# A decoder trunk in split float32: every second weight chunk's remainder is formed by ScalarE and an accumulating GpSimd DMA instead of VectorE

## The chip, the cores and the metric

The kernel runs on one core of one Trainium2 chip. The metric is the device time of one execution in microseconds (us); the time of a kernel is the median of its runs. Line numbers (L153) are those of the kernel before, unless a row is said to be of the changed kernel.

## What is computed

Four pre-norm residual layers over 512 tokens of width 1024 (pool, conv, attention, pool), each with a branch of width 2048 and a SiLU gate, then a final RMS norm. Cut to what matters:

```python
for i in range(4):                       # pool, conv, mla, pool
    xn = rms_norm(x, norm[i])
    x = x + mixer[i](xn, ...)            # every mixer ends in (y * silu(z)) @ w_out
return rms_norm(x, final_norm)

# pool_mixer:  u, z = split(xn @ w_in, 2); trailing means over 2/4/8/16 tokens minus u,
#              per group @ w_grp, * scale, * silu(z), @ w_out
# conv_mixer:  b, c, h, z = split(xn @ w_in, 4); y = b * conv3(c * h); (y * silu(z)) @ w_out
# mla_mixer:   q, kv latents, rotary key, z from xn @ w_in; 16 heads of causal softmax
#              attention; (o * silu(z)) @ w_out
```

All of it is float32, and nearly all of the work is in the matrix products with the weights.

## The kernel before, in words

Activations lie feature-major in SBUF: 8 tiles of 128 features x 512 tokens. TensorE multiplies in a rounded float32 format (float32r), so each operand is split in two: a rounded half `h` and a remainder `l = raw - h`, and each product is three matmuls, `h*h`, `h*l` and `l*h` (`mm3`, L156 to L159). In the rows the weights are `wh` and `wl`, and the activations `xh`, `xl` or `yh`, `yl`; a row `pz<-xh,wl` writes the PSUM tile pz.

The weights are streamed in chunks of 128 x 1024. `wchunk` (L142) loads one chunk over SP's queue into a raw buffer `wr`, ScalarE writes the rounded half `wh` (L152), VectorE subtracts for the remainder `wl` (L153). There are three buffers each of `wr`, `wh` and `wl`. A chunk feeds 24 matmuls of 128x512. 222 chunks go this way. Another 22, inside attention, are called with `pool=True`: GpSimd does both steps (L149, L150).

I number the 222 chunks from 0 in the order of the code: 0 to 37 are the first pool layer, 38 to 53 its output projection, 54 to 133 the conv layer and its projection, 134 to 155 the input projection of the attention layer, 156 to 169 its output projection, 170 to 221 the last pool layer and its projection.

Beside the splits, VectorE multiplies the norm's factor into the PSUM tiles (L280), forms the mixers' products and splits the activations together with ScalarE (L136, L139). GpSimd forms the running sums of the pool layers (L299: one to four additions for each channel tile, by its window), sums the squares for the norms (L180), and in attention scales the probabilities (L548) and splits those 22 chunks.

The order of instructions on each engine is set by a scheduler, from the program and its own idea of durations; each engine then takes its instructions in that order. The code places one tile by hand: the last gate tile of the attention layer (chunk 155) is issued after the rotary queries, the values and the first head's queries and keys of the first group (`qrope(0)`, `values(0)`, `stage_a(0)`, then `ly.tile`). Its split stands on ScalarE behind the rounded halves of the rotary queries, `qah` and `qbh`.

Of the kernel before, what the change touches and what calls it, by code (L numbers as in the profile page):

```python
# [12 lines left out]
AF = mybir.ActivationFunctionType  # L13
ALU = mybir.AluOpType
# [19 lines left out]
CH = 1024  # L34
WARM = 8

# attention: at which step (head of the group, place within the head's step) the next group's
# values and rotary queries are computed, for the first group and the others
VALUES_AT = ((0, 3), (2, 0), (2, 0))
ROTARY_AT = ((2, 1), (1, 1), (1, 1))  # L40
SPLIT_Y_FROM = 10

# columns of the per-partition parameter array
PC = {}
_n = 0
for _name, _w in (
# [5 lines left out]
    _n += _w  # L52
NPAR = _n

# columns of the constant array
C_ID, C_MASK, C_INV, C_FREQ, C_SIGN, NCON = 0, 128, 640, 704, 705, 706


# [1 line left out]
def trunk_kernel(ctx: ExitStack, tc: tile.TileContext, a):  # L60
# [20 lines left out]
    def f(t):  # L81
        return t.bitcast(F32)

# [1 line left out]
    con = cp.tile([P, NCON], F32, name="con")  # L85
    par = cp.tile([P, NPAR], F32, name="par")
    xt = [xp.tile([P, S], F32, name=f"x{m}") for m in range(KD)]
# [41 lines left out]
    def pcol(name, i):  # L129
        return par[:, PC[name][0] + i : PC[name][0] + i + 1]  # L130

# [1 line left out]
    def split(src, s, eng="act", w=S):  # L133
        h, l = ut(s + "h", F32R, w), ut(s + "l", F32R, w)
        if eng == "act":
# [6 lines left out]
    def wchunk(src, width=CH, pool=False, raw=None):  # L142
        if raw is None:
            raw = wp.tile([P, CH], F32, tag="wr", name=nm("wr"))[:, :width]
            nc.sync.dma_start(raw, src)
        h = wp.tile([P, CH], F32R, tag="wh", name=nm("wh"))[:, :width]
        l = wp.tile([P, CH], F32R, tag="wl", name=nm("wl"))[:, :width]
        if pool:
            nc.gpsimd.tensor_scalar(out=h, in0=raw, scalar1=1.0, scalar2=1.0, op0=ALU.mult, op1=ALU.mult)  # L149
            nc.gpsimd.tensor_tensor(out=l, in0=raw, in1=f(h), op=ALU.subtract)  # L150
        else:
            nc.scalar.activation(h, raw, AF.Copy)  # L152
            nc.vector.tensor_tensor(out=l, in0=raw, in1=f(h), op=ALU.subtract)  # L153
        return h, l

    def mm3(out, ah, al, bh, bl, first, last):  # L156
        nc.tensor.matmul(out, ah, bh, start=first, stop=False)  # L157
# [1 line left out]
        nc.tensor.matmul(out, al, bh, start=False, stop=last)  # L159

    def mtile(out, wh, wl, xs, k0=0, kn=KD, ktot=KD, stride=P, off=0):
        """out += sum over kn k-tiles of w[k].T @ xs[k0 + k]"""
        for k in range(kn):
            c = slice(k * stride + off, k * stride + off + P)
            mm3(out, wh[:, c], wl[:, c], *xs[k0 + k], first=(k0 + k == 0), last=(k0 + k == ktot - 1))

    class Stats:
        """sum of squares over the feature tiles, then the norm's factor of each token"""

        def __init__(self, dim, n):  # L170
            self.dim, self.n, self.i, self.sum = dim, n, 0, None
# [11 lines left out]
                self.parts = split(self.sum, "ss")  # L183

        def rows(self):
            """the factor of token 128 i + p in column i of partition p"""
            st = ps("st")
            for t in self.parts:
                nc.tensor.matmul(st, ones, t, start=(t is self.parts[0]), stop=(t is self.parts[1]))
            v = sp.tile([P, NT], F32, tag="sv", name=nm("sv"))  # L190
            for i in range(NT):
                d = sp.tile([P, P], F32, tag="sd", name=nm("sd"))
                nc.vector.tensor_tensor_reduce(
                    out=d, in0=st[:, i * P : (i + 1) * P], in1=ident, scale=1.0 / self.dim, scalar=EPS,
                    op0=ALU.mult, op1=ALU.add, accum_out=v[:, i : i + 1],
                )
            r = sp.tile([P, NT], F32, tag="sr", name=nm("sr"))
            nc.gpsimd.tensor_tensor(out=r, in0=v, in1=mhalf, op=ALU.pow)
            return r
# [19 lines left out]
            return R  # L219

    class XNorm:
        """xg = x * gain, split, with the statistics of x"""

        def __init__(self, gain):
            self.gain, self.xs, self.st = gain, [], Stats(D, KD)
# [8 lines left out]
                self.st.add(xt[m])  # L234

    class Layer:
        """A layer's first tiles wait in PSUM until the norm's factor is there."""

        def __init__(self, xn, at=(1, 3)):
            self.xn, self.R, self.n, self.posts, self.at = xn, None, 0, [], at  # L240
# [22 lines left out]
        mtile(o, wh, wl, ys, k0=8 * hf, kn=8, ktot=KI)  # L263

    def out_proj(w, ys, gain, o0=None, after=()):
        """x += y @ w, feature-major; the next layer's XNorm (o0: the first half of its first tile)"""
        xn = XNorm(gain)
        for m in range(KD):
            if m == 0 and o0 is not None:
                o = o0  # L270
            else:
                o = ps("o")
                out_half(w, ys, m, 0, o, after=after if m < 2 else ())
            out_half(w, ys, m, 1, o, pool=m == 0 and o0 is not None)
            nc.vector.tensor_tensor(out=xt[m], in0=o, in1=xt[m], op=ALU.add)
            xn.add(m)
        return xn
# [1 line left out]
    def tmul(dst, src, R):  # L279
        nc.vector.tensor_tensor(out=dst, in0=src, in1=R, op=ALU.mult)  # L280

# [1 line left out]
    def pool_layer(j, xn, mid=None, pre=(), at=(1, 3)):  # L283
        win, wg = a[f"pool_in{j}"], a[f"pool_grp{j}"]
        ys = []
# [49 lines left out]
                mid(g)  # L335
        return ys

# [1 line left out]
    def conv_layer(xn):  # L339
        win = a["conv_in"]  # L340
        ys = []
# [37 lines left out]
            ly.tile(win[3 * KI + i], "pz", post_z)  # L379
        return ys  # L380

# [1 line left out]
    def rope_tables():  # L383
        pi = cp.tile([P, S], I32, name="posi")
        nc.sync.dma_start(pi, a["positions"].broadcast_to((P, S)))
# [26 lines left out]
        nc.scalar.activation(cos, t, AF.Sin, scale=-1.0, bias=hp)  # L412
        return cos, sin

# [1 line left out]
    def mla_layer(xn, cos, sin):  # L416
        win = a["mla_in"]
        ly = Layer(xn)
# [7 lines left out]
            (skv if len(lat) <= 2 else sq_).add(t)  # L426

        def post_kr(pl):
            # rotary key, rows [k1, k2, k1, k2]
            kr0, ksw = ut("kr0"), ut("ksw")  # L430
            tmul(kr0, pl, ly.R)
            for q in range(4):
                s = q ^ 1
                nc.sync.dma_start(ksw[32 * q : 32 * q + 32, :], kr0[32 * s : 32 * s + 32, :])
            nc.vector.tensor_tensor(out=kr0, in0=kr0, in1=cos, op=ALU.mult)
            nc.vector.scalar_tensor_tensor(out=ksw, in0=ksw, scalar=con[:, C_SIGN : C_SIGN + 1], in1=sin, op0=ALU.mult, op1=ALU.mult)
            nc.vector.tensor_tensor(out=kr0, in0=kr0, in1=ksw, op=ALU.add)
            kr.extend(split(kr0, "kr"))
# [181 lines left out]
            split_y()  # L620
        return ys, o0, [i.ins for i in last.values()]

# [1 line left out]
    xn = XNorm("pool_norm0")  # L624
    w0, pre = {}, [ps("pu") for _ in range(2)]

# [38 lines left out]
    ys, o0, after = mla_layer(xn, cos, sin)  # L665
    xn = out_proj(a["mla_out"], ys, "pool_norm1", o0, after)

    # last layer: the output projection goes token-major
    xtok = {}

    def turn(g):
# [21 lines left out]


    def token_tile(pos, half, i):
        """the PSUM tiles and columns of token tile i (the very last one comes in two)"""
        if half == 0 or i < NT - 1:
            return [(pos[i], slice(0, S))]
        return [(pos[i + q][:, : S // 2], slice(q * (S // 2), (q + 1) * (S // 2))) for q in range(2)]
# [67 lines left out]


def _layout(i):
    """The inputs in the order in which the chip streams them."""  # L770
    i = {k: np.asarray(v) for k, v in i.items()}

    def cols(v):
        return v.reshape(-1, P).T

    def w_in(w):
        k, n = w.shape
        return w.reshape(k // P, P, n // P, P).transpose(2, 1, 0, 3).reshape(n // P, P, k)

    def w_out(w):  # L780
        return w.reshape(2, 8, P, 8, P).transpose(3, 0, 2, 1, 4).reshape(8, 2, P, CH)

    out = {
        "xT": i["x"][0].T,
        "positions": i["positions"],
        "con": _constants(),
        "par": np.concatenate(
            [cols(i["pool_norm"][0]), cols(i["pool_norm"][1]), cols(i["conv_norm"][0]), cols(i["mla_norm"][0]),
             cols(i["mla_q_norm"][0]), cols(i["mla_kv_norm"][0]), cols(i["pool_scale"][0]), cols(i["pool_scale"][1]),
             *[cols(i["conv_w"][0][q]) for q in range(3)]], axis=1),  # L790
        "final_norm": i["final_norm"][None, :],
        "conv_in": w_in(i["conv_w_in"][0]),
        "conv_out": w_out(i["conv_w_out"][0]),
        "mla_out": w_out(i["mla_w_out"][0]),
        "pool_out0": w_out(i["pool_w_out"][0]),
        "pool_out1": i["pool_w_out"][1].reshape(8, 2, P, 2, S).transpose(3, 0, 2, 1, 4).reshape(2, 8, P, CH),
    }
    for j in range(2):
        out[f"pool_in{j}"] = w_in(i["pool_w_in"][j])
        out[f"pool_grp{j}"] = i["pool_w_grp"][j].reshape(4, 4, P, 2, 2 * P).transpose(0, 3, 2, 1, 4).reshape(4, 2, P, CH)  # L800
    w = i["mla_w_in"][0]
    rope = w[:, QL + KVL : QL + KVL + DR]
    out["mla_in"] = w_in(np.concatenate([w[:, QL : QL + KVL], w[:, :QL], rope, rope, w[:, QL + KVL + DR :]], axis=1))
    q = i["mla_w_q_up"][0].reshape(3, P, H, DN + DR)
    nope = q[..., :DN].reshape(3, P, 8, 2 * P).transpose(2, 1, 0, 3).reshape(8, P, 768)
    rot = q[..., DN:].reshape(3, P, 4, 4, 2, 32).transpose(2, 1, 0, 4, 3, 5).reshape(4, P, 768)
    out["q_up"] = np.concatenate([nope, rot], axis=0)
    kv = i["mla_w_kv_up"][0].reshape(2, P, H, 2, P)
    for n, e in (("k_up", 0), ("v_up", 1)):
        out[n] = kv[:, :, :, e].reshape(2, P, 4, S).transpose(2, 1, 0, 3).reshape(4, P, CH)  # L810
    return {k: np.ascontiguousarray(v) for k, v in out.items()}
# [17 lines left out]
```

## Time and profile before

| | |
|---|---|
| time, median of 3 runs | 1506.08 us (1506.01 to 1506.9) |
| span of the profiled execution, first to last instruction | 1504.8 us |
| profiled execution's own time outside its span | not given; the median of the runs lies 1.3 us above the span |
| TensorE matmuls busy | 1490.4 us, 6712 matmuls |
| VectorE, ScalarE, GpSimd busy | 779.5, 495.0, 305.2 us |
| mean granted TensorE clock | 0.995 |

How to read the rows. A group row has line, engine, operation, written and read tiles (buffer numbers left out), shapes, count, then busy us and mean ns of one, then the idle time of the engine just before them and what ended it. A timeline row has the start (us from the span's start), the duration in us, engine, line, operation, tiles, count, and in brackets the idle time before it and what ended that. A row of waits has the waiting engine and line, the one it waited for, the us in total, how often, and the longest. PE is TensorE's matmuls, PEld its weight loads, DVE VectorE, ACT ScalarE, POOL GpSimd, SP the queue that issues loads. A row of windows has the stretch, its length, the busy time of the five engines with the number of their instructions, then the granted clock, the mean share of the DMA engines that was busy, and GB/s.

### The profile page before, as it was taken

What the parts mean: (1) busy time and instruction counts of PE and PEld (TensorE: products, weight loads), DVE (VectorE), ACT (ScalarE), POOL (GpSimd) and SP (SyncE); (2) the same over time, 40 slices, a digit from 0 to 9 for tenths busy, and PEclk for the clock granted to TensorE, in tenths of its full rate; (3) what the DMA queues carried; (4) which work ended last, traced back from release to release, by engine and by line L of the source; (5) the groups of instructions that cost most, each with busy time, mean ns of one, the idle gap of its engine ahead of it and who ended that gap; (6) DMA issues with size and microseconds to landing.
All of it is one profiled execution on the core that took longest, in us unless ns stands there. A gap on an engine that the chain in (4) does not pass through costs nothing.

```text
span 1504.8 us, 17426 instructions
## 1 busy us (share of the span) xinstructions
PE 1490.4 (99%) x6712; PEld 1221.1 (81%) x6712; DVE 779.5 (52%) x1250; ACT 495.0 (33%) x772; POOL 305.2 (20%) x312
## 2 busy tenths in 40 slices
PE   9999999999999999999999999899999999999998
PEld 7888888888888888888888878788888888888887
DVE  4665454335554555556345545666643455545442
ACT  5333233322222222223232424445632233333331
POOL 2223320111000000000101035445711111134010
PEclk9999999999999999999999999999999999999999
DMA  6233323233333333333233232223123333323331
GB/s 214 85 98 98 98 93 92 96 97 95 90 96 98 99 86 97 98 98 98 88 95 105 82 94 69 67 75 81 43 85 98 91 92 98 88 95 99 100 111 56
DMA packets 42659, 140.49 MB, mean 93 GB/s; under 512 B 5584, under 2 KB 5584, under 8 KB 42576
## 3 DMA queue, kind: packets, MB, share of 16 engines
q1 hardware_dynamic: 41712, 137.81, 30.3%
q10 hardware_dynamic: 864, 1.57, 0.3%
q8 instruction: 52, 0.85, 0.2%
q14 instruction: 31, 0.25, 0.1%
HBM read 132.80 MB, written 2.10 MB: 90 GB/s over the span
## 4 chain that ended last, share of the span: by engine, by line
PE 97%; DVE 1%; issue 0%; ACT 0%; DMA 0%; SPq 0%; POOLq 0%; POOL 0%; ACTq 0%
PE pz L159 8%; PE pz L157 8%; PE pz L158 8%; PE o L157 6%; PE o L158 6%; PE o L159 6%; PE pu L159 4%; PE pu L157 4%; PE pu L158 4%; PE pb L159 2%; PE pc L159 2%; PE ph L159 2%; PE pm L158 2%; PE pm L159 2%; PE pm L157 2%; PE ph L157 2%
## 5 line engine op out<-in xcount | busy, mean ns | idle before, releaser
L152 ACT ACTIVATE wh<-wr 128x1024 fp32r<-128x1024 f32 x222 | 235.4, 1060 | 699.7 <-issue 183.1
L153 DVE TENSOR_TENSOR wl<-wr,wh 128x1024 fp32r<-128x1024 f32 x222 | 298.5, 1345 | 226.3 <-ACT wh L152 226.1
L159 PE MATMUL pz<-xh,wl 128*128 128x512 f32 x512 | 201.8, 394 | 0.3 <-DVE wl L153 0.3
L157 PE MATMUL pz<-xh,wh 128*128 128x512 f32 x512 | 201.5, 394 | 0.0
L158 PE MATMUL pz<-xl,wh 128*128 128x512 f32 x512 | 200.9, 392 | 0.0
L157 PE MATMUL o<-yh,wh 128*128 128x512 f32 x384 | 151.4, 394 | 0.0
L159 PE MATMUL o<-yh,wl 128*128 128x512 f32 x384 | 151.2, 394 | 0.0
L158 PE MATMUL o<-yl,wh 128*128 128x512 f32 x384 | 151.1, 393 | 0.0
L159 PEld LDWEIGHTS pz<-xh,wl 128*128 128x128 f32 x512 | 96.1, 188 | 22.9 <-DVE wl L153 0.7
L158 PEld LDWEIGHTS pz<-xl,wh 128*128 128x128 f32 x512 | 96.3, 188 | 22.5
L157 PEld LDWEIGHTS pz<-xh,wh 128*128 128x128 f32 x512 | 96.1, 188 | 21.9
L159 PE MATMUL pu<-xh,wl 128*128 128x512 f32 x255 | 100.6, 396 | 0.3 <-DVE wl L630 0.3
L157 PE MATMUL pu<-xh,wh 128*128 128x512 f32 x255 | 100.6, 399 | 0.0
L158 PE MATMUL pu<-xl,wh 128*128 128x512 f32 x255 | 100.5, 395 | 0.0
L180 POOL TENSOR_TENSOR sq<-sq,sq 128x512 f32<-128x512 f32 x25 | 42.0, 1681 | 264.6 <-ACT sq L175 264.2
L299 POOL TENSOR_TENSOR s<-u 128x527 f32<-128x527 f32 x32 | 37.4, 1169 | 267.8 <-DVE u L280 247.3
L280 DVE TENSOR_TENSOR sz<-pz,R 128x512 f32<-128x512 f32 x64 | 42.4, 687 | 87.7 <-PE pz L159 87.7
L159 PEld LDWEIGHTS o<-yh,wl 128*128 128x128 f32 x384 | 72.2, 188 | 16.7
L158 PEld LDWEIGHTS o<-yl,wh 128*128 128x128 f32 x384 | 72.2, 188 | 16.5
L157 PEld LDWEIGHTS o<-yh,wh 128*128 128x128 f32 x384 | 72.2, 188 | 16.4
L367 POOL TENSOR_TENSOR yb<-yb,R 128x512 f32<-128x512 f32 x16 | 20.7, 1293 | 309.9 <-DVE yb L366 309.9
L299 POOL TENSOR_TENSOR s<-s 128x525 f32<-128x525 f32 (+2 forms) x48 | 63.9, 1331 | 3.8
(229 smaller groups left out, 2839.8 us busy)
## 6 DMA issues: line engine op xcount, KB each, us to landing
wr<-in_conv_in SPq DMA_DIRECT2D x64, 512.0 KB, 3.6
wr<-in_pool_in SPq DMA_DIRECT2D x62, 512.0 KB, 3.7
wr<-in_pool_out SPq DMA_DIRECT2D x32, 512.0 KB, 3.7
wr<-in_mla_in SPq DMA_DIRECT2D x22, 512.0 KB, 3.6
wr<-in_pool_grp SPq DMA_DIRECT2D x16, 512.0 KB, 3.6
wr<-in_conv_out SPq DMA_DIRECT2D x16, 512.0 KB, 3.7
wr<-in_mla_out SPq DMA_DIRECT2D x16, 512.0 KB, 3.7
wr<-in_q_up SPq DMA_DIRECT2D x12, 384.0 KB, 3.1
```

Source lines behind the costliest of these rows:

```text
L152: nc.scalar.activation(h, raw, AF.Copy)
L153: nc.vector.tensor_tensor(out=l, in0=raw, in1=f(h), op=ALU.subtract)
L157: nc.tensor.matmul(out, ah, bh, start=first, stop=False)
L158: nc.tensor.matmul(out, ah, bl, start=False, stop=False)
L159: nc.tensor.matmul(out, al, bh, start=False, stop=last)
L180: eng.tensor_tensor(out=self.sum, in0=self.sum, in1=sq, op=ALU.add)
L280: nc.vector.tensor_tensor(out=dst, in0=src, in1=R, op=ALU.mult)
L299: nc.gpsimd.tensor_tensor(out=nx[:, lo:], in0=cur[:, lo:], in1=cur[:, lo - d : S + PAD - d], op=ALU.add)
L367: nc.gpsimd.tensor_tensor(out=y, in0=y, in1=ly.R, op=ALU.mult)
```

## The change

`wchunk` counts its calls. For every second chunk (1, 3, ... 221; 111 of the 222), ScalarE writes the rounded half as before, then the same copy with the sign turned into `wl` (`scale=-1.0`), and GpSimd issues a DMA that adds the raw chunk onto `wl` in SBUF: `-h + raw` is the remainder. VectorE has no part in these chunks. The even chunks and those with `pool=True` are split as before.

```diff
         if pool:
             nc.gpsimd.tensor_scalar(out=h, in0=raw, scalar1=1.0, scalar2=1.0, op0=ALU.mult, op1=ALU.mult)
             nc.gpsimd.tensor_tensor(out=l, in0=raw, in1=f(h), op=ALU.subtract)
+        elif acc[0] % 2:
+            acc[0] += 1
+            nc.scalar.activation(h, raw, AF.Copy)
+            nc.scalar.activation(l, raw, AF.Copy, scale=-1.0)
+            nc.gpsimd.dma_start(f(l), raw, accum_op=ALU.add)
         else:
+            acc[0] += 1
             nc.scalar.activation(h, raw, AF.Copy)
             nc.vector.tensor_tensor(out=l, in0=raw, in1=f(h), op=ALU.subtract)
         return h, l
+
+    acc = [0]
```

In the changed kernel the lines behind are eight higher: an even chunk has its rounded half on L158 and its subtraction on L159, an odd one L153 (rounded half), L154 (sign-turned copy) and L155 (the DMA); the matmuls are L165 to L167. Several comments fall away too.

The scheduler orders every engine anew. ScalarE before, around the split of chunk 155 (`wh_6380`; qah and qbh are the rotary queries' rounded halves, vh, qh and kh those of values, queries and keys):

```order
L136 ACTIVATE qah_6263<-t_1122_6255 128x512
L136 ACTIVATE qbh_6267<-t_1123_6256 128x512
L152 ACTIVATE wh_6380<-wr_6378 128x1024
L136 ACTIVATE vh_6304<-pv_6297 128x512
L136 ACTIVATE vh_6315<-pv_6308 128x512
```

And ScalarE at the same place of the changed kernel (chunk 155 is `wh_6457`, `wl_6458`):

```order
L136 ACTIVATE qah_6340<-t_1122_6332 128x512
L136 ACTIVATE qbh_6344<-t_1123_6333 128x512
L154 ACTIVATE wl_6458<-wr_6455 128x1024
L153 ACTIVATE wh_6457<-wr_6455 128x1024
L136 ACTIVATE vh_6381<-pv_6374 128x512
```

The split keeps its place behind `qbh`, with the sign-turned copy ahead of the rounded half. On GpSimd the DMA of that chunk stands behind the last of the four `pool=True` splits that come before it, in the changed kernel:

```order
L149 TENSOR_SCALAR wh_6420<-wr_6418 128x768
L150 TENSOR_TENSOR wl_6421<-wr_6418,wh_6420 128x768
L149 TENSOR_SCALAR wh_6426<-wr_6424 128x1024
L150 TENSOR_TENSOR wl_6427<-wr_6424,wh_6426 128x1024
L155 DMA wl_6458<-wr_6455 128x1024
L149 TENSOR_SCALAR wh_6568<-wr_6566 128x1024
```

Between those two splits (the ends of the piece) there was nothing before. The second place is the first pool layer, GpSimd before, the running sums of two neighbouring channel tiles (`u_747` is the input of a tile, `s` its sums):

```order
L299 TENSOR_TENSOR s_617<-s_615 128x525
L293 MEMSET u_747 128x16
L299 TENSOR_TENSOR s_750<-u_747 128x527
L299 TENSOR_TENSOR s_752<-s_750 128x525
L293 MEMSET u_794 128x16
```

And there in the changed kernel (`wl_853` is chunk 13, `wl_922` chunk 15, `u_752` the same input):

```order
L155 DMA wl_853<-wr_850 128x1024
L301 MEMSET u_752 128x16
L307 TENSOR_TENSOR s_755<-u_752 128x527
L155 DMA wl_922<-wr_919 128x1024
L307 TENSOR_TENSOR s_757<-s_755 128x525
L301 MEMSET u_800 128x16
```

The transfer of chunk 15 stands behind the first addition of this tile. The transfer of chunk 11 stands in the same way behind the second addition of an earlier one. TensorE's order differs in a few places only. The one that matters here is the group mix at the end of the first pool layer, TensorE before (`plh_1654` is the last channel tile, pm the products of the mix, which begins 13 matmuls ahead of the first row with `plh_1654`):

```order
L158 MATMUL pm_1819<-pll_1414,wh_1796 128x512
L159 MATMUL pm_1819<-plh_1413,wl_1797 128x512
L157 MATMUL pm_1819<-plh_1464,wh_1796 128x512
L157 MATMUL pm_1800<-plh_1654,wh_1796 128x512
L158 MATMUL pm_1819<-pll_1465,wh_1796 128x512
```

And in the changed kernel, where the same tile is `plh_1670`:

```order
L165 MATMUL pm_1882<-plh_1618,wh_1858 128x512
L166 MATMUL pm_1882<-pll_1619,wh_1858 128x512
L167 MATMUL pm_1882<-plh_1618,wl_1859 128x512
L165 MATMUL pm_1818<-plh_1670,wh_1814 128x512
L165 MATMUL pm_1837<-plh_1670,wh_1814 128x512
L165 MATMUL pm_1863<-plh_1670,wh_1858 128x512
L165 MATMUL pm_1882<-plh_1670,wh_1858 128x512
```

All matmuls with the last channel tile have moved to the end of the mix, 36 matmuls behind its start.

## The prediction

> **What bounds the kernel now.** I read the page's engine totals first, then what TensorE waits for, then single chunks on the timeline. The totals:
>
> ```profile
> span 1504.8 us, 17426 instructions
> PE 1490.4 (99%) x6712; PEld 1221.1 (81%) x6712; DVE 779.5 (52%) x1250; ACT 495.0 (33%) x772; POOL 305.2 (20%) x312
> ```
>
> TensorE is busy for all but 14.4 us of the span. Whatever leaves VectorE (52%) shortens nothing unless TensorE waits for it, so the next view is the waits of TensorE alone:
>
> ```profile
> PE s L534 <- ACT kh L136: 4.9, 1, 4.9
> PE warm L127 <- DVE dummy L89: 1.4, 1, 1.4
> PE pu L655 <- DVE xl L231: 0.6, 1, 0.6
> PE pu L159 <- DVE wl L630: 0.3, 1, 0.3
> PE pz L159 <- DVE wl L153: 0.3, 1, 0.3
> ```
>
> Only the last of these rows is line 153, the line that the change removes from half the chunks: one wait of 0.3 us. The largest, 4.9 us in attention, ends on line 136, which the change leaves alone, and no changed chunk lies near it (the chunks there are split on GpSimd with pool=True). So the change can save some 0.3 us, and the question is what it puts at risk: how long before its first use is a remainder finished today? One ordinary odd chunk, number 53 (the last of pool_out0), ScalarE, VectorE and TensorE rows of the timeline:
>
> ```profile
> 303.88 1.06 ACT L152 ACTIVATE wh<-wr 128x1024 fp32r<-128x1024 f32 x1 [3.35 <-issue]
> 304.98 1.23 DVE L153 TENSOR_TENSOR wl<-wr,wh 128x1024 fp32r<-128x1024 f32 x1 [3.65 <-ACT wh L152]
> ...
> 314.95 0.40 PE L157 MATMUL o<-yh,wh 128*128 128x512 f32 x1
> 315.18 0.40 PE L158 MATMUL o<-yl,wh 128*128 128x512 f32 x1
> 315.42 0.39 PE L159 MATMUL o<-yh,wl 128*128 128x512 f32 x1
> ```
>
> ScalarE may start once TensorE has left the third-last chunk (three buffers of each kind); TensorE reaches the new remainder two chunks later, at 315.42: 11.5 us after ScalarE's start, of which 2.3 are used (303.88 to 306.21). The same distance holds through the projections; I looked for the odd chunks where it is shorter.
>
> **What the change does, term by term.** 111 of 222 remainders leave VectorE: 111 x 1.345 us = 149 us by the first row here, which lie beside TensorE's work and save nothing. 111 copies of the second row's kind are added, 111 x 1.06 = 118 us, on an engine that is 33% busy. And 111 transfers are queued on GpSimd, each behind its copy.
>
> ```profile
> L153 DVE TENSOR_TENSOR wl<-wr,wh 128x1024 fp32r<-128x1024 f32 x222 | 298.5, 1345 | 226.3 <-ACT wh L152 226.1
> L152 ACT ACTIVATE wh<-wr 128x1024 fp32r<-128x1024 f32 x222 | 235.4, 1060 | 699.7 <-issue 183.1
> ```
>
> Call A the time from the transfer's issue on GpSimd to its landing. An ordinary chunk then needs 1.06 + 1.06 + 0.1 (my allowance for the hand-over) + A of its 11.5 us, so an A up to 9.3 us is hidden by the two chunks that TensorE works on meanwhile; beyond that TensorE waits. The raw buffer is held until the transfer lands, but its next load needs only 3.6 us and is wanted three chunks (3 x 24 matmuls of 0.23, 16.6 us) after the start: that breaks at 16.6 - 2.2 - 3.6 = 10.8, later than 9.3.
>
> No row has an accumulating transfer or one from GpSimd. The nearest are these (KB each, median us to landing):
>
> ```profile
> wr<-in_conv_in SPq DMA_DIRECT2D x64, 512.0 KB, 3.6
> wr<-in_q_up SPq DMA_DIRECT2D x12, 384.0 KB, 3.1
> qrs<-qah SPq DMA_DIRECT2D x16, 64.0 KB, 2.0
> ```
>
> The lower bound is 2.0 us, an SBUF to SBUF copy of an eighth of the size. From 384 to 512 KB a load grows by 0.5 us, so 512 KB are about 2.0 us of moving and 1.6 of fixed time. An addition reads 512 KB twice and writes it once: with the two reads in series 1.6 + 2 x 2.0 = 5.6 us. Three whole passes of a load, 3 x 3.6 = 10.8 us, are the upper bound. I take A = 5.6 as an estimate, nearest to the load row with its moving part doubled.
>
> The Trainium skill bears on this: "Collectives: The Full Stack" (The bandwidth ceiling) says that the adding in a DMA is free and the second source read halves the rate, and "DMA: Bandwidth & Descriptors" (Anatomy of one DMA) gives 2.0 us plus bytes over 436 GB/s for a GpSimd-issued transfer. For 1.05 MB read that is an estimate of 4.4 us, and the sum below would come to 1510.5; its formula gives 3.2 us for a plain 512 KB where the trace's loads take 3.6, and no row here shows an addition.
>
> With A = 5.6 the ordinary chunks stay hidden. Where is the cover thinner? **Chunk 155**, the last gate tile of the attention layer, is split late, because on ScalarE it stands behind the rotary queries:
>
> ```profile
> 895.86 0.63 ACT L136 ACTIVATE qbh<-t 128x512 fp32r<-128x512 f32 x1 [1.36 <-DVE t L503]
> 896.40 1.05 ACT L152 ACTIVATE wh<-wr 128x1024 fp32r<-128x1024 f32 x1
> ...
> 897.48 1.23 DVE L153 TENSOR_TENSOR wl<-wr,wh 128x1024 fp32r<-128x1024 f32 x1 [0.26 <-ACT wh L152]
> ...
> 898.76 0.50 PE L159 MATMUL pz<-xh,wl 128*128 128x512 f32 x1 [0.31 <-DVE wl L153]
> ```
>
> It arrives exactly when used. In the changed order ScalarE writes the sign-turned copy first (896.40 to 897.45), then the rounded half (to 898.5). GpSimd has nothing before the transfer at that time:
>
> ```profile
> 889.97 2.72 POOL L150 TENSOR_TENSOR wl<-wr,wh 128x1024 fp32r<-128x1024 f32 x1
> 904.00 1.05 POOL L149 TENSOR_SCALAR wh<-wr 128x1024 fp32r<-128x1024 f32 x1 [11.32 <-PE pz L158]
> ```
>
> So it is issued at 897.55 and lands at 897.55 + A; TensorE, whose order here is the same, moves from 898.76 by A - 1.2 = **4.4 us**. What stands behind it in TensorE's order waits with it. The GpSimd split at 904.00 waits for this tile and moves along; so do the rotary work and the 4.9 us wait of the next group, which begin from TensorE's own matmuls.
>
> A pause this long has a second price, the clock. The windows around the existing 4.9 us wait (PE busy, then the other engines, the granted clock third from the end):
>
> ```profile
> 940.00:945.00 5.00, 1.02 (x10) 0.78 (x8) 4.30 (x4) 0.76 (x2) 4.92 (x3) 0.90 0.08 21
> 945.00:950.00 5.00, 4.03 (x9) 2.73 (x10) 4.42 (x8) 2.15 (x6) 0.87 (x1) 0.50 0.33 79
> 950.00:955.00 5.00, 5.00 (x31) 4.65 (x30) 2.83 (x13) 2.45 (x8) 2.08 (x4) 0.92 0.44 105
> ```
>
> While TensorE worked again, the clock was at half for 4.03 us of the middle window and short by 8% of the last: 2.0 + 0.4 = 2.4 us lost. A pause of 4.7 us (4.4 and the 0.31 there already) is nearly as long as that one, and one case is all the trace has; I take half the price, **1.2 us**.
>
> "TensorE: Matmul & The Clock Gate" in the Trainium skill (Part 1: The HAM clock gate) says that the clock halves after one whole free-running window of about 3.4 us without work; the 4.9 us wait agrees. By it an estimate of (4.7 - 3.4) / 3.4, some 4 in 10, would hit, near the half that I took.
>
> **Chunk 15**, a gate tile of the first pool layer, is the second thin place. GpSimd now has its transfer behind the first addition of a running sum, whose input comes late:
>
> ```profile
> 93.26 1.06 ACT L152 ACTIVATE wh<-wr 128x1024 fp32r<-128x1024 f32 x1 [0.96 <-PE pz L158]
> ...
> 99.01 1.06 POOL L299 TENSOR_TENSOR s<-u 128x527 f32<-128x527 f32 x1 [16.43 <-PE pz L159]
> ...
> 104.78 0.40 PE L159 MATMUL pz<-xh,wl 128*128 128x512 f32 x1
> ```
>
> Issue at 100.07 instead of 95.5, used at 104.78: 4.7 us of cover, so a wait of 5.6 - 4.7 = **0.9 us**. The next are chunk 159 (split at 1112.92, used at 1121.46: 8.54 - 2.22 = 6.3 us of cover) and chunk 11 (behind an addition that ends at 76.19, used at 82.64: 6.4); both hold at 5.6.
>
> ```profile
> 1112.92 1.06 ACT L152 ACTIVATE wh<-wr 128x1024 fp32r<-128x1024 f32 x1 [2.64 <-PE o L158]
> 1121.46 0.39 PE L159 MATMUL o<-yh,wl 128*128 128x512 f32 x1
> 75.13 1.06 POOL L299 TENSOR_TENSOR s<-s 128x525 f32<-128x525 f32 x1
> 82.64 0.40 PE L159 MATMUL pu<-xh,wl 128*128 128x512 f32 x1
> ```
>
> The other way round, GpSimd's additions queue behind transfers that wait for their copies. That reaches TensorE only at the end of a pool layer, where today the sums of the last channel tile end at 216.5 and the group mix begins at 220.65; the matmuls of that tile now stand 36 matmuls (8.3 us at 0.23 each) into the mix, so some 9 us of delay would be covered after the 3 us that VectorE and ScalarE need. I cost it at nothing.
>
> ```profile
> 214.07 2.43 POOL L299 TENSOR_TENSOR s<-s 128x521 f32<-128x521 f32 x2
> 220.65 0.39 PE L157 MATMUL pm<-plh,wh 128*128 128x512 f32 x1
> ```
>
> More traffic on the DMA engines is no bound by itself: the queue that carries the weights fills 30.3% of them, and 111 transfers of twice a load's reads add about as much again.
>
> ```profile
> q1 hardware_dynamic: 41712, 137.81, 30.3%
> ```
>
> **Sum.** 4.4 + 1.2 + 0.9 = 6.5 us. The profiled execution spans 1504.8 us; the median of the runs, 1506.08, lies 1.3 above it, for what lies around the span. 1504.8 + 6.5 + 1.3 = **1512.6 us**. A measurement of this kernel can tell about 0.2% (3.0 us) from no change.
>
> **Rivals.**
> - *A quick addition, no change to be told.* If A is 2.0 to 3.9 us, chunk 155 costs 0.8 to 2.7 and the pause is under 3.1, well short of the one that cost the clock, so I add no price for it: 1506.9 to 1508.8. For it speaks that both ends are in SBUF, as in the 2.0 us row; against it that 512 KB from memory take 3.6. This ends on the other side, not slower. Decided at A = 3.9.
> - *A slow addition that sets the pace.* Above 9.3 us ordinary chunks wait too. A chunk that waited gives the next odd one more room (its buffer was released before the wait), so about every second of the 111 pays: at the bound of 10.8, 55 x 1.5 = 83 us, with some 20 of the thin places about 1610. For it: three passes could be made one after the other; against it: the load row needs only 2.0 us of moving per pass.
> - *Faster.* The 4.9 us wait ends on a chain of VectorE steps of which one takes 2.76 us, where the group before takes 0.67 for the same (the chain that ended last, start and length):
>
> ```profile
> 894.57 0.67 DVE qal L139
> 940.22 2.76 DVE qal L139
> ```
>
>   If the shift undoes that stretch, the wait gives back some 2 us and its 2.4 us of clock. With A = 2.0 (0.8 us) that is 1506.1 + 0.8 - 4.4 = 1502.5. Against it: that chain and the GpSimd splits beside it both start from TensorE, so their overlap should repeat.
>
> **How the numbers follow.** Forecast (A from 3.9 to 9.3) 0.63, quick 0.18, slow 0.15, faster 0.04. The forecast's upper end at A = 9.2: 8.0 at chunk 155, 4.5 at 15, 2.9 at 159, 2.8 at 11, and the clock's 2.4 at both longest pauses: 23.0 us, 1529.1. The range goes from the quick case's 1506.9 to there, 1507 to 1529; the slow and the faster case, about 2 in 10, are left out. Faster by over 0.2%: 0.04; within 0.2%: 0.18; slower: 0.63 + 0.15 = 0.78.
>
> **What would show it.** Right: the waits of TensorE hold one new row near 898 us, on line 159 for a transfer of wl, of about 4.7 us; the DMA issues show wl from GpSimd at 5 to 6 us to landing; near 105 us a wait of about 1 us; elsewhere none. Wrong: a landing time below 3.9 or above 9.3; waits on ordinary chunks, on the sums of the pool layers, or on ScalarE's rounded halves; or a 4.9 us wait that has changed its length.

## The result, and the profile after

The changed kernel takes **1516.00 us** (median of 3 runs, 1515.41 to 1516.73) where the kernel before takes 1506.08. The ratio is 1.0064, with a 95% interval of 1.0044 to 1.0083: 9.9 us slower. The forecast was 1512.6. From here on, lines are those of the changed kernel.

The totals and two of the DMA queues of the page of the changed kernel:

```profile
span 1514.7 us, 17696 instructions
PE 1492.3 (99%) x6712; PEld 1223.1 (81%) x6712; DVE 619.0 (41%) x1139; ACT 599.6 (40%) x883; POOL 391.6 (26%) x423
...
q1 hardware_dynamic: 41712, 137.81, 27.8%
q0 software_dynamic: 15984, 58.20, 20.4%
```

VectorE lost 160 us of work, ScalarE gained 105 and GpSimd 86; none of that is the cost, as the runs below show. The waits of TensorE (waiting line, what it waited for, us in total, times, longest):

```profile
PE s L542 <- ACT kh L136: 4.9, 1, 4.9
PE pz L167 <- DMA wl<-wr: 4.1, 1, 4.1
PE warm L127 <- DVE dummy L89: 1.5, 1, 1.5
PE pu L661 <- DVE wh L637: 0.7, 1, 0.7
PE pz L165 <- ACT wh L153: 0.4, 1, 0.4
```

111 transfers, and one wait for one of them. It is chunk 155, on the timeline of ScalarE, GpSimd and TensorE:

```profile
896.36 1.04 ACT L154 ACTIVATE wl<-wr 128x1024 fp32r<-128x1024 f32 x1
897.31 1.04 ACT L153 ACTIVATE wh<-wr 128x1024 fp32r<-128x1024 f32 x1
...
897.70 0.89 POOL L155 DMA_DIRECT2D wl<-wr  x1 [5.06 <-ACT wl L154]
...
898.40 0.50 PE L165 MATMUL pz<-xh,wh 128*128 128x512 f32 x1 [0.44 <-ACT wh L153]
898.73 0.40 PE L166 MATMUL pz<-xl,wh 128*128 128x512 f32 x1
903.22 0.79 PE L167 MATMUL pz<-xh,wl 128*128 128x512 f32 x1 [4.09 <-DMA wl<-wr]
903.81 0.63 PE L165 MATMUL pz<-xh,wh 128*128 128x512 f32 x1
```

The copy, the issue, 5.5 us from 897.70 to the first matmul at 903.22, and then matmuls of 0.63 to 0.79 us where the row before the wait has 0.40: the clock has halved. The windows behind the wait (PE busy first, the granted clock third from the end):

```profile
900.00:905.00 5.00, 1.78 (x4) 1.49 (x5) 2.54 (x5) 1.26 (x3) 0.00 (x0) 0.60 0.78 161
905.00:910.00 5.00, 5.00 (x17) 3.95 (x16) 0.00 (x0) 0.00 (x0) 0.00 (x0) 0.71 0.53 149
```

1.78 us at half speed lose 0.9, 5.00 us at 0.71 lose 1.45: together about 2.3 us of clock. So this one place costs some 6.4 us.

The rest is behind the last matmul. The last output is issued on ScalarE's queue; first the row of before, whose span ends at 1504.8, then that of after, which ends at 1514.7:

```profile
1501.28 0.34 ACTq L752 DMA_DIRECT2D out<-fo  x1
```

```profile
1507.42 0.34 ACTq L760 DMA_DIRECT2D out<-fo  x1
```

3.5 us from there to the end before, 7.3 us after: 3.8 us more, with no kernel instruction in them. The trace names it. Every engine meets the others at the end, and GpSimd arrives last, because its closing drain instruction takes 7.95 us where it took 1.03. The rows of before and after (the line that the end of the program is put down to, POOLq for GpSimd's sequencer, how many, the shortest, median and longest in ns, first and last start):

```profile
L825 POOLq DRAIN  x3: 39/77/1034, 1499.5 to 1504.5; - x3
```

```profile
L833 POOLq DRAIN  x3: 34/102/7952, 1505.7 to 1514.1; - x3
```

In both kernels the last of the other engines, SP, arrives 4.5 us after this drain begins (1504.07 against 1499.53 before, 1510.20 against 1505.67 after). So 1.03 us of drain were hidden, and 7.95 stand out by 3.4; the other 0.4 of the 3.8 lie behind the meeting, and their cause is not shown.

6.4 and 3.8 are 10.2; smaller shifts of both signs take 0.3 back. Matched by their number in TensorE's order, the matmuls of the changed kernel start 0.9 us early at 118 us of the kernel before, 1.2 late at 672 and level with it at 895, just ahead of chunk 155. So the transfers up to there cost nothing on balance. The DMA issues (KB each, median us to landing) give the price that had no row before:

```profile
wl<-wr POOLq DMA_DIRECT2D x111, 512.0 KB, 4.5
wr<-in_conv_in SPq DMA_DIRECT2D x64, 512.0 KB, 3.8
wr<-in_pool_in SPq DMA_DIRECT2D x62, 512.0 KB, 4.3
```

### The profile page after: what moved, and what is told of

Its sections match the earlier page's. It is cut to its first block, busy times and chain, and to the rows that moved or that the text cites. A ratio compares the mean times of both kernels' runs of the same rounds, so it can differ in the third digit from the quotient of the medians.

```text
span 1514.7 us, 17696 instructions
## 1 busy us (share of the span) xinstructions
PE 1492.3 (99%) x6712; PEld 1223.1 (81%) x6712; DVE 619.0 (41%) x1139; ACT 599.6 (40%) x883; POOL 391.6 (26%) x423
## 3 DMA queue, kind: packets, MB, share of 16 engines
q0 software_dynamic: 15984, 58.20, 20.4%
## 5 line engine op out<-in xcount | busy, mean ns | idle before, releaser
L158 ACT ACTIVATE wh<-wr 128x1024 fp32r<-128x1024 f32 x111 | 117.6, 1060 | 309.7 <-issue 271.2
L155 POOL DMA_DIRECT2D wl<-wr x111 | 97.2, 876 | 551.2 <-ACT wl L154 512.1
L153 ACT ACTIVATE wh<-wr 128x1024 fp32r<-128x1024 f32 x111 | 117.6, 1059 | 306.9 <-issue 123.9
L167 PE MATMUL pz<-xh,wl 128*128 128x512 f32 x512 | 202.6, 396 | 4.1 <-DMA wl<-wr 4.1
L165 PE MATMUL pz<-xh,wh 128*128 128x512 f32 x512 | 202.1, 395 | 0.4 <-ACT wh L153 0.4
L159 DVE TENSOR_TENSOR wl<-wr,wh 128x1024 fp32r<-128x1024 f32 x111 | 137.6, 1240 | 118.8 <-ACT wh L158 118.7
L165 PE MATMUL o<-yh,wh 128*128 128x512 f32 x384 | 151.1, 394 | 0.0
L167 PE MATMUL o<-yh,wl 128*128 128x512 f32 x384 | 150.9, 393 | 0.0
L154 ACT ACTIVATE wl<-wr 128x1024 fp32r<-128x1024 f32 x111 | 115.8, 1043 | 13.7 <-PE po L166 13.7
L167 PEld LDWEIGHTS pz<-xh,wl 128*128 128x128 f32 x512 | 96.6, 189 | 26.7 <-DMA wl<-wr 4.5
L165 PEld LDWEIGHTS pz<-xh,wh 128*128 128x128 f32 x512 | 96.6, 189 | 22.7 <-ACT wh L153 0.9
L165 PE MATMUL pu<-xh,wh 128*128 128x512 f32 x255 | 100.2, 397 | 0.0
L167 PE MATMUL pu<-xh,wl 128*128 128x512 f32 x255 | 100.1, 394 | 0.0
L167 PEld LDWEIGHTS o<-yh,wl 128*128 128x128 f32 x384 | 72.2, 188 | 16.8
L165 PEld LDWEIGHTS o<-yh,wh 128*128 128x128 f32 x384 | 72.1, 188 | 16.7
L283 DVE TENSOR_TENSOR x<-o,x 128x512 f32<-128x512 f32 x24 | 16.6, 692 | 167.7 <-PE o L167 167.7
```

What stands on the lines that cost most here:

```text
L154: nc.scalar.activation(l, raw, AF.Copy, scale=-1.0)
L155: nc.gpsimd.dma_start(f(l), raw, accum_op=ALU.add)
```

## The experiments

The theory: chunk 155 costs 6.4 us (wait and clock), the closing drain 3.8, and the other 110 transfers nothing. The main rival: the cost is spread over all transfers. In each run the kernel before was timed on the same chip; its median there was 1506.52 us for the first four runs below, 1505.91 for the next four and 1506.27 for the last four.

### Chunk 155 kept on VectorE

```diff
-        elif acc[0] % 2:
+        elif acc[0] % 2 and acc[0] != 155:
```

> As changed, but chunk 155 alone is split on VectorE again. Theory: the change costs 4.2 us of wait and about 2.2 us of clock at chunk 155, and 3.8 us behind the last output, where GpSimd's closing drain takes 7.95 us instead of 1.03; the other 110 transfers cost nothing. Then the wait on line 167 near 898 us is gone and the time falls by 6.4 from 1516.0 to 1509.6, with the long closing drain still there. Rival (the 9.9 us are spread over the 111 transfers, by contention with the loads): 110/111 of the cost stays, about 1515.9. Rival (the closing drain is a consequence of the late chunk): about 1506.

Measured: **1509.39 us**, ratio 1.0019 (1.0010 to 1.0028). With one chunk of 111 changed back, 2.9 us are left of the 9.9 (1509.39 against 1506.52). The wait is gone, the drain is still 7.87 us. The theory holds; a cost spread evenly over the transfers, which would have left 1515.9, is excluded.

### Chunk 155 alone

```diff
-        elif acc[0] % 2:
+        elif acc[0] == 155:
```

> Only chunk 155 goes by ScalarE and the accumulating DMA; all others as before. Theory: this one transfer holds nearly the whole cost: 4.2 + 2.2 at TensorE and 3.8 at the end, 1506.1 + 10.2 = 1516.3. Rival (the closing drain grows with the number of transfers): the 3.8 shrinks to 3.8/111, 1512.5. Rival (cost spread over all transfers): 1506.2.

Measured: **1513.74 us**, ratio 1.0050 (1.0037 to 1.0062). This is neither 1516.3 nor 1506.2. The wait is there in full:

```profile
PE pz L167 <- DMA wl<-wr: 4.3, 1, 4.3
...
PE pz L165 <- ACT wh L153: 0.5, 1, 0.5
```

But the drain takes 1.13 us and the end 3.5: the drain does grow with the transfers, as the first rival had it. 7.2 us are the price of the wait (4.3 and 0.5, less the 0.3 that was there before), of the clock, and about half a microsecond of small shifts. The 7.2 us of chunk 155 alone and the 2.9 us of all the others add up to 10.1, close to the 9.9 of the whole change.

### Chunk 3 alone

```diff
-        elif acc[0] % 2:
+        elif acc[0] == 3:
```

> Only chunk 3 goes by the accumulating DMA, some 1450 us before the end and well covered. Theory: no matmul waits for it, but the closing drain of GpSimd is as long as with 111 transfers: 1506.1 + 3.8 = 1509.9. Rival (the drain is long only because transfers are recent at the end, or many): 1506.1, drain about 1 us.

Measured: 1506.81 us, ratio 1.0001 (0.9993 to 1.0010), drain 1.13 us. The theory of a fixed price at the end falls. A single well-covered transfer costs nothing that can be told.

### The sign-turned copies without the DMA

```diff
-            nc.gpsimd.dma_start(f(l), raw, accum_op=ALU.add)
+            nc.vector.tensor_tensor(out=l, in0=raw, in1=f(l), op=ALU.add)
```

> As changed, with ScalarE's sign-turned copy, but VectorE adds the raw chunk onto it in place of the DMA. It measures the 111 extra copies of ScalarE alone. Theory: they cost only at chunk 155, where the remainder is ready at about 897.45 + 0.1 + 1.24 = 898.8 as before and the rounded half is 0.4 us late: 1506.1 to 1506.6, closing drain 1 us. Rival (the longer row of ScalarE delays chunks elsewhere, and the slow drift of 2 us over the conv layer comes from it): 1508 or more.

Measured: 1506.65 us, ratio 1.0001 (0.9992 to 1.0010), drain as before. 111 extra copies on ScalarE, 104 us of work, are free; of what the theory named, only the 0.4 us wait for the rounded half of chunk 155 shows.

### A plain copy in place of the addition

```diff
-            nc.gpsimd.dma_start(f(l), raw, accum_op=ALU.add)
+            nc.gpsimd.dma_start(f(l), raw)
```

> As changed, chunk 155 included, but the transfers copy the raw chunk over the sign-turned copy and add nothing, so the remainder is left out: wl holds the raw chunk. It prices the addition. If the second read takes time, the landing falls from 4.5 us to that of a load, 3.6 to 4.3, and the wait at chunk 155 from 4.1 to about 3.2: 1516.0 - 0.9 = 1515.1, or 1512.9 if the shorter pause spares the clock its 2.2. Rival (the addition is free, and the 4.5 are what any 512 KB transfer of GpSimd takes): landing, wait and time unchanged, 1516.0.

Measured: 1516.69 us, ratio 1.0073 (1.0058 to 1.0088). The forecasts of 1515.1 and 1512.9 are missed. The time alone would say that the addition is free; the trace says otherwise. Its queue and its issues:

```profile
q0 software_dynamic: 15984, 58.20, 9.7%
...
wl<-wr POOLq DMA_DIRECT2D x111, 512.0 KB, 2.9
```

The same bytes hold the DMA engines half as long (9.7% against 20.4%), and a transfer lands 1.6 us sooner (2.9 against 4.5). The Trainium skill's rule on the second source read ("Collectives: The Full Stack", The bandwidth ceiling: twice the read traffic for each byte written) agrees with both rows. The wait at chunk 155 is 2.7 us, 1.4 less, but two things take that back. The closing drain is 10.12 us, longer than with the addition, and the end 9.4 instead of 7.3. And the shorter pause did not spare the clock:

```profile
900.00:905.00 5.00, 3.13 (x7) 2.48 (x8) 2.58 (x5) 1.31 (x3) 0.00 (x0) 0.60 0.56 160
905.00:910.00 5.00, 5.00 (x17) 3.97 (x16) 0.03 (x1) 0.00 (x0) 0.13 (x1) 0.72 0.49 132
```

After 2.7 us of pause the clock is at 0.60 and 0.72, as after 4.1. The shorter pause even pays more: TensorE works for 3.13 us of the first window instead of 1.78, and loses 1.6 there and 1.4 in the second, 3.0 us instead of 2.3. "TensorE: Matmul & The Clock Gate" in the Trainium skill (Part 1: The HAM clock gate) asks for an idle window of about 3.4 us. Here a pause of 2.7 was enough, with one of 0.44 and two matmuls just ahead, so the measurement decides. The three differences sum to 1.4 us more, yet the span is only 0.2 longer: behind the 4.9 us wait in attention the lead of the matmuls over the changed kernel grows from 0.7 to 2.0 us.

### A second transfer behind each first

```diff
-        elif acc[0] % 2:
+        elif acc[0] % 2 and acc[0] != 155:
...
             nc.gpsimd.dma_start(f(l), raw, accum_op=ALU.add)
+            nc.gpsimd.dma_start(f(l), f(l))
```

> As changed with chunk 155 on VectorE, and behind each of the 110 adding transfers a second one that copies the remainder onto itself, so that a remainder lands after 4.5 + 0.1 + some 4.4 = 9.0 us. It tests the cover of 9.3 us that the prediction gave to an ordinary chunk. Theory: the conv layer still shows no wait of TensorE for a remainder; chunk 159 (cover 6.3) and chunk 11 (6.4) wait some 2.7 and 2.6, and the pool layers lose a little by a GpSimd that waits for the first transfer: 1509.4 + 5 to 12 = 1514 to 1521. Rival (the cover is really 8 us or less): about every second of some 100 ordinary chunks waits 1 us or more, over 1560.

Measured: **1566.86 us**, ratio 1.0411 (1.0394 to 1.0428). The forecast of 1514 to 1521 is missed, and by the time alone the rival won. But the second transfer was slower than I had put it, 5.3 us and not 4.4, as the issues show; beside them the first waits of TensorE:

```profile
wl<-wr POOLq DMA_DIRECT2D x110, 512.0 KB, 4.6
wl<-wl POOLq DMA_DIRECT2D x110, 512.0 KB, 5.3
```

```profile
PE pz L168 <- DMA wl<-wl: 15.0, 19, 3.2
PE po L167 <- DMA wl<-wl: 7.3, 2, 5.9
PE s L543 <- ACT kh L136: 4.8, 1, 4.8
PE o L168 <- DMA wl<-wl: 4.6, 10, 0.8
PE pm L168 <- DMA wl<-wl: 3.4, 2, 1.7
PE pu L168 <- DMA wl<-wl: 3.2, 4, 1.5
```

One ordinary chunk of the conv layer, ScalarE, GpSimd and TensorE rows of its timeline:

```profile
392.66 1.06 ACT L153 ACTIVATE wh<-wr 128x1024 fp32r<-128x1024 f32 x1 [1.49 <-PE pc L167]
...
394.96 0.87 POOL L155 DMA_DIRECT2D wl<-wr  x1 [5.99 <-ACT wl L154]
399.86 0.56 POOL L156 DMA_DIRECT2D wl<-wl  x1 [4.02 <-DMA wl<-wr]
...
404.97 0.50 PE L168 MATMUL pz<-xh,wl 128*128 128x512 f32 x1 [0.61 <-DMA wl<-wl]
```

404.97 - 394.96 = 10.0 us to landing against a cover of 9.3, and TensorE waits 0.61. The nineteen waits on `pz` average 0.8. So the cover of 9.3 us is right within a few tenths (10.0 less the wait is 9.4), and the time is what a landing of 10 does to it: the waits on these transfers sum to 34 us of the 54.7 by which the span has grown. PE is busy 1506.7 us instead of 1490.4. Little of that is the clock: its mean is 0.994 against 0.995, some 1559.5 x 0.006 - 1504.8 x 0.005 = 1.8 us. The first matmul behind a wait has a longer row (0.50 above, where the usual is 0.39), which is part of the rest; what else is in it is not shown. Above its kernel before, this run lies 60.9 us, the one with the 110 first transfers alone 2.9.

### How the closing drain grows: none late, late ones only, every fourth, all

```diff
-        elif acc[0] % 2:
+        elif acc[0] % 2 and acc[0] < 210 and acc[0] != 155:
```

> As changed, but chunk 155 and the six odd chunks of the last projection (211 to 221) are split on VectorE: 104 transfers, the last some 60 us before the end. The run with chunk 3 alone showed no long closing drain, that with 110 transfers did: number or nearness? If nearness to the end makes the drain long: drain about 1 us, 1506 (1505 to 1506.5). If the number does: as with 110 transfers, 1509.4.

```diff
-        elif acc[0] % 2:
+        elif acc[0] % 2 and acc[0] >= 210:
```

> Only the six odd chunks of the last projection (211 to 221) go by the adding transfer. If nearness to the end makes the closing drain long: 1506.5 + 3.4 = 1509.9, drain about 8 us. If the number does: 1506.5, drain 1 us.

Measured: **1509.00 us**, ratio 1.0020 (1.0010 to 1.0030), drain 7.38, and 1506.77 us, ratio 1.0006 (0.9996 to 1.0015), drain 1.54. It is the number (or the bytes, since all transfers have one size), not the nearness to the end.

```diff
-        elif acc[0] % 2:
+        elif acc[0] % 4 == 1:
```

> Every fourth chunk (1, 5, ... 221; 56 of 222, chunk 155 not among them) goes by the adding transfer, the others as before. So far GpSimd's closing drain took 1.03 us without transfers, 1.13 with 1, 1.54 with 6, 7.38 with 104, 7.87 with 110: some 0.062 us for each. The last output lands 4.7 us after the drain begins, so the drain is hidden up to (4.7 - 1.0) / 0.062 = 59 transfers. Theory: 56 give a drain of 4.5 us and cost nothing: 1506 (1505 to 1506.8). Rival (each transfer costs its 0.03 us of the 3.4 whatever the drain is beside): 1506.4 + 1.7 = 1508.1.

Measured: **1510.26 us**, ratio 1.0024 (1.0015 to 1.0034), a miss of both forecasts. The drain is 5.63 us, not 4.5: 0.082 us for each of the 56, so that the end takes 4.7 us, 1.2 more than before. The other 2.8 us are not at the end. Some 2 of them come in the conv layer: over its b, c and h tiles the starts of consecutive matmuls lie 232.2 ns apart on average, in the kernel before 230.8; no row shows a wait and the granted clock is 1.00 in both. ScalarE's copies are not the reason (230.6 in the run that had them without the DMA), and it does not grow with the number of transfers (231.9 with 104 to 111, 231.4 with 221). From 672 to 895 us of the kernel before it is the other way round: 231.8 there, and 230.5 with 110 transfers, so that run gets the time back. What this is stays open.

```diff
-        elif acc[0] % 2:
+        elif acc[0] != 155:
```

> All 222 chunks but 155 go by ScalarE and the adding transfer; VectorE splits only chunk 155. Twice the transfers: if the drain grows by 0.062 us for each, it takes 1.03 + 221 x 0.062 = 14.7 us, and the time is 1509.4 + 6.9 = 1516.3. If the drain clears only what an earlier wait or a full queue has not cleared (220 transfers, half of them waited for by GpSimd, left a drain of 4.5 us), it is 4 to 5 us and the time about 1506. Either way the remainders land in about 5 us of their 9.3 and TensorE waits for none; a rival (DMA engines or ScalarE too busy): waits on ordinary chunks, over 1525.

Measured: **1510.04 us**, ratio 1.0026 (1.0015 to 1.0036). VectorE is down to 33%, the drain is **1.79 us** and the end 3.6 us after the last output's issue. Both forecasts of time and of drain are missed, and a transfer takes 6.2 us, not about 5. Its issues, and the two waits on transfers:

```profile
wl<-wr POOLq DMA_DIRECT2D x221, 512.0 KB, 6.2
wr<-in_conv_in SPq DMA_DIRECT2D x64, 512.0 KB, 4.9
```

```profile
PE o L167 <- DMA wl<-wr: 1.3, 1, 1.3
...
PE pu L167 <- DMA wl<-wr: 0.4, 1, 0.4
```

The 1.3 us are at 1125.75, on chunk 159, which the prediction named as the next thin place with a cover of 6.3 us; the 0.4 are at 21.53, at the start of the kernel. Together they are 1.7 of the 3.8 us that this run lies above its kernel before; no row of waits names the rest. The runs together (transfers of GpSimd, its closing drain, and the time from the last output's issue to the end of the span, us):

| transfers | drain | issue to end |
|---|---|---|
| 0 | 1.03 | 3.5 |
| 1 (chunk 155) | 1.13 | 3.5 |
| 2 (the next section) | 1.21 | 3.5 |
| 6 | 1.54 | 3.5 |
| 56 | 5.63 | 4.7 |
| 104 | 7.38 | 6.4 |
| 110 | 7.87 | 6.9 |
| 111 | 7.95 | 7.3 |
| 111, plain copies | 10.12 | 9.4 |
| 110 and 110 second ones | 4.53 | 3.5 |
| 221 | 1.79 | 3.6 |

Up to 56, and for the plain copies, it is 0.08 to 0.10 us for each transfer; at 104 to 111 adding ones 0.06; with 220, half of them waited for by GpSimd, 0.02; and with 221 only 0.8 us in all are left. That fits a list of finished transfers that the drain has to clear and that is cleared during the run too, once it is long enough; but no run shows the clearing itself, so that is only argued. Some 4.5 us of drain are hidden, since SP arrives that long after the drain begins: the 5.63 us of 56 transfers stand out by 1.1 and the 7.38 of 104 by 2.9, near the 1.2 and 2.9 by which their ends are longer.

### A version that beats both: the head 4 chunks of attention

The 4.9 us wait in attention is untouched by the change. In the trace of before, VectorE's rows of the rotary chain and GpSimd's beside them:

```profile
939.29 0.93 DVE L501 TENSOR_TENSOR t<-qr,cos 128x512 f32<-128x512 f32 x1
940.14 2.84 DVE L139 TENSOR_TENSOR qal<-t,qah 128x512 fp32r<-128x512 f32 x1
942.90 1.30 DVE L503 TENSOR_TENSOR t<-t,qr 128x512 f32<-128x512 f32 x1
```

```profile
939.77 2.67 POOL L150 TENSOR_TENSOR wl<-wr,wh 128x1024 fp32r<-128x1024 f32 x1
942.40 1.27 POOL L149 TENSOR_SCALAR wh<-wr 128x768 fp32r<-128x768 f32 x1
```

`qal` ends 0.5 us after GpSimd's subtraction does, as if it had waited for it. So the transfer was put where it relieves GpSimd, on the two chunks that are split there, and nowhere else:

```diff
-        elif acc[0] % 2:
+        elif pool is None:
...
-                hold["q"] = wchunk(wq[h // 2], 768, pool=True)
+                hold["q"] = wchunk(wq[h // 2], 768, pool=(True if h != 4 else None))
...
-                hold["k"] = wchunk(wk[h // 4], pool=True)
+                hold["k"] = wchunk(wk[h // 4], pool=(True if h != 4 else None))
```

> The kernel before, and only the two chunks of head 4 in attention (its queries and keys, until now split on GpSimd beside VectorE's rotary steps) go by ScalarE and the adding transfer. Theory: VectorE's subtraction of 2.84 us at 940 and its neighbours fall back to 0.7 each, ScalarE reaches the keys' rounded half at about 943.4 instead of 945.25, the 4.9 us wait shrinks to some 2.5 to 3 and may keep or lose its 2.4 us of clock: 1501.2 to 1504.4. Rival (the chain is not set by the GpSimd split beside it, or ScalarE's four extra copies take what is won): 1506.

Measured: **1503.77 us**, ratio 0.9983 (0.9974 to 0.9992), 2.5 us faster than before. VectorE's rows, and what is left of the wait:

```profile
938.28 0.69 DVE L139 TENSOR_TENSOR qal<-t,qah 128x512 fp32r<-128x512 f32 x1
938.89 0.68 DVE L511 TENSOR_TENSOR t<-t,qr 128x512 f32<-128x512 f32 x1
940.75 2.17 DVE L139 TENSOR_TENSOR qbl<-t,qbh 128x512 fp32r<-128x512 f32 x1 [1.17 <-ACT qbh L136]
```

```profile
941.74 0.68 PE L542 MATMUL s<-kh,qh 128*128 128x512 f32 x2 [0.87 <-ACT kh L136]
943.58 0.46 PE L542 MATMUL s<-kh,qh 128*128 128x256 f32 x1 [1.17 <-DVE ql L139]
```

`qal` takes 0.69 us. 4.9 us of wait have become 0.9 and 1.2; the 1.2 are left because the next GpSimd split (1.81 us from 940.56) now meets `qbl`, which takes 2.17. The Trainium skill, "SBUF — State Buffer" (SBUF: two separate sides), says that VectorE and GpSimd share a port pair that one of them locks for a whole instruction; both stretched rows end right after a GpSimd subtraction, which agrees.

The control: the same two chunks split by ScalarE and VectorE (`False` in place of `None` in both lines).

> The kernel before, and only the two chunks of head 4 are split by ScalarE and VectorE, like the ordinary ones. The control for the run before: the GpSimd work beside the rotary chain is gone too, but VectorE has 2 us more in the chain. Theory: wait of about 2.7 to 3.5 in place of 4.9, 1502 to 1505. Rival (GpSimd's split is not what stretches VectorE): the wait grows by 2 us, 1508.

Measured: 1505.26 us, ratio 0.9993 (0.9984 to 1.0002). The wait is 2.6 and 0.7 us and the clock still falls, to 0.71 and 0.60 in the windows from 940 to 950. The control's time cannot be told from that of the kernel before, but its wait is shorter too. So it was GpSimd's split beside the rotary chain that made the wait long, and the move that adds nothing to VectorE helps more.

## Why the prediction was right, and what it missed

- **Ordinary chunks hidden by a cover of 9.3 us:** right. No ordinary chunk waits at a landing of 4.5 us, and at 6.2 only one of the first, 0.4 us; at 10.0 the waits are about the difference.
- **A = 5.6 at chunk 155, a wait of 4.4:** right, in part by luck. 5.5 and 4.1 there (5.7 and 4.3 with this transfer alone), and the first matmul on the remainder moved from 898.76 to 903.22, by 4.5. But A stood for every transfer, and the median is 4.5, below the 5 to 6 that it named as its sign. At chunk 155 a transfer takes some 1.0 to 1.2 us more than the median, a plain copy too (4.1 against 2.9); why is not shown. With the median, or with the estimate of 4.4 from "DMA: Bandwidth & Descriptors" (Anatomy of one DMA) in the Trainium skill, the wait would have come out some 1.2 too short.
- **A wait for ScalarE's rounded half:** one of its own signs of being wrong, and it came, 0.4 us at chunk 155. The prediction had that half ready at 898.5; in the kernel before its first matmul starts at 897.82, which the prediction left out. Here the longer wait behind it hides it.
- **The clock at half its price, 1.2:** the step that halved it failed. It cost 2.3, the whole price, and the plain copies paid 3.0 after a pause of 2.7. In the same way the quick rival's claim that a pause under 3.1 us costs no clock is wrong.
- **Chunk 15, 0.9 us:** it cost nothing. The step that failed kept GpSimd's first addition at 99.01, with the transfer behind it. Now its input comes earlier, and the transfer is issued at 94.69, some 9 us ahead of its use. Whether VectorE's relief or the new order of the engines did that is not separated (with ScalarE's copies and no DMA the addition starts at 96.63):

```profile
92.99 1.06 POOL L307 TENSOR_TENSOR s<-u 128x527 f32<-128x527 f32 x1 [7.84 <-DVE u L288]
94.69 0.88 POOL L155 DMA_DIRECT2D wl<-wr  x1 [0.64 <-ACT wl L154]
```

- **The sum had no term for the end.** "What lies around the span" and the stretch behind the last matmul were taken over from the kernel before. The end made 3.8 us of the 9.9, of which 3.4 are the drain; this is the largest error. Without those 3.8 us the time would be 1512.2, near the 1512.6, but there 1.1 too little for the clock and 0.9 too much for chunk 15 nearly cancel. That the time lies in the range of 1507 to 1529 in spite of a missing term owes to the width of the range.
- **Pool sums, ScalarE and DMA traffic at nothing:** right. The copies alone are free, and the loads of weights land up to 0.6 us later without being waited for.
- **The rivals:** the slow addition is what the run with two transfers looks like, and its waits are about as dear as the rival said: 34 us at 0.7 past the cover, 49 for each us, where the rival had 83 at 1.5, 55 for each; the run as a whole lost more, 60.9. The faster one did not come: the 4.9 us wait stayed as it was, since its cause, GpSimd's split beside the rotary chain, stayed.

The sum again: 4.1 of wait, 2.3 of clock, 0 at chunk 15, 3.8 at the end and -0.3 of shifts, 9.9 us, where the prediction had 4.4 + 1.2 + 0.9 = 6.5.

## What to carry to other kernels

Work that leaves an engine saves nothing where nobody waits for it, as here with VectorE at 52%, and work that becomes longer costs nothing while it stays inside its cover; so look for the one place among the 111 where the cover is thin, and leave that place alone. When a change brings an engine or a queue something it did not do before, price the end of the kernel too, where every engine has to finish. The same tool can pay elsewhere: two transfers placed where they take GpSimd off VectorE's way won 2.5 us, where 111 placed by parity lost 9.9.

## What was unexpected of the hardware

- GpSimd's closing drain grows with its transfers, 0.08 us each up to 56 (1.03 to 5.63 us), to 7.95 with 111 adding ones and 10.12 with 111 copying ones, and is short again (1.79) with 221.
- A pause of 2.7 us, with one of 0.44 just ahead, halves TensorE's clock as one of 4.1 does, at a price of 3.0 and 2.3 us. In the run with two transfers in attention, pauses of 0.9 and 1.2 us within 3 us still brought it to 0.87 and 0.78 in the windows from 940 to 950.
- An adding transfer of 512 KB within SBUF lands in 4.5 us and a copying one in 2.9, both issued by GpSimd in less than 1 us (0.88 and 0.57).
